# Retention chunks: the group norm moved to POOL and ScalarE one chunk later, PSUM shared out anew, ten modulation rows moved into the loop

## The chip, the core and the metric

The kernel runs on one core of a Trainium2 chip. Its engines work side by side, each through its own instructions in the order in which they were written, and wait for each other by semaphores: PE (TensorE, matrix products out of SBUF into PSUM), DVE (VectorE, elementwise work), ACT (ScalarE, scale, bias, function and copies), POOL (GpSimd, elementwise work in SBUF), and SP, whose queue issues most of the DMAs. PSUM has eight banks of 128 x 512 float32. The metric is the device time of one execution in microseconds; lower is better.

## The reference, cut to what matters

The program is one decoder block on 1024 tokens with a width of 1024: a norm, a token mixer (retention with a gate, and dilated attention), and an MLP. All of it is float32. The change is in the retention, with four heads, chunks of 128 tokens, keys 256 wide and values 512 wide:

```
def step(state, inp):
    qi, ki, vi = inp
    s = jnp.einsum('bhid,bhjd->bhij', qi, ki) * inner_decay[None]
    o = (jnp.einsum('bhij,bhje->bhie', s, vi)
         + jnp.einsum('bhid,bhde->bhie', qi, state) * q_decay[None, :, :, None])
    state = (state * chunk_decay[None, :, None, None]
             + jnp.einsum('bhjd,bhje->bhde', ki * k_decay[None, :, :, None], vi))
    return state, o
...
mu = jnp.mean(ro, axis=-1, keepdims=True)
var = jnp.mean(jnp.square(ro - mu), axis=-1, keepdims=True)
ro = ((ro - mu) * lax.rsqrt(var + GN_EPS)).transpose(0, 2, 1, 3).reshape(B, S, RET_V_W)
ro = (ro * gn_g.astype(jnp.float32) + gn_b.astype(jnp.float32)).astype(h.dtype)
ret_out = (jax.nn.silu(rg) * ro) @ w_ret_out
```

The modulation rows (`mod = silu(c) @ w_ada + b_ada`, 48 columns of 128) are sums of a row of `w_ada` times a vector, made on DVE.

## The kernel before

A float32 product is made of three products of rounded parts: each operand is split into a high part (a rounding copy on ACT) and a low part (a subtraction on DVE), and `mm3` (lines 203 to 211) runs low times high, high times low and high times high, so that one product shows as matmuls of L207, L209 and L211. Each splitting of a 128 x 1024 weight is one ACT copy (L197) and one DVE subtraction (L198).

The order of the instructions is the order of the program text on each engine; nothing reorders them. Steps are run one after the other by `Steps.run`. A step has a list of loads and what is to be done with each when it has come (`wsplit`: split a weight; `mod_load`: one modulation row). SP issues the loads up to three ahead of their use. A chunk's body gets a function `ahead`; where it calls `ahead(2)`, the loads of the next step are prepared, so the splitting and the modulation rows of step g + 1 stand in the engines' order where chunk g calls it.

The stages that matter are `queries_keys` and `values` (lines 1259 and 1384), which end near 712 us, then 32 calls of `chunk(h, c)` (line 715) for head h and chunk c, numbered g = 8 h + c, until near 980 us, then the attention steps. During `queries_keys` and `values`, `mod_turn` (line 1243) loads and sums `NV` = 32 modulation rows in turn, between the other work.

In a chunk TensorE does, in this order: six matmuls for the new state (`kv`, not for c = 7); `RG[h][c] - 1` steps of the gate's projection (`rg_mm`, six matmuls a step; eight steps make a tile of the gate); `s_kt(g + 1)`, the next chunk's scores (`sT`) and transposed keys (`kT`); the chunk's output `o` (nine matmuls, three for c = 0); `on_T(g - 1)`, four transposes (`oT`) of the chunk before, after its norm; one more step of the gate. Around it: DVE brings the state up to date (L745) and takes its low part (L750); ACT takes the high part (L749). In `s_kt` ACT copies the scores out (L652), DVE adds and multiplies by the decay (L653, L654), ACT rounds them (L664), and keys are split (L663, L666). At the end of a chunk DVE takes mean and variance of `o` in PSUM (L772, L773), scales the variance (L774), POOL raises it to -1/2 (L775), DVE scales again (L776) and norms `o` into `onm` (L778). `jit_qk` splits queries and keys on ACT and POOL (L616, L617). For h > 0 and c < 4, `u_final` (line 681) finishes one quarter of the head before: two ACT instructions (L688), one DVE product with the gate (L690), and a store on SP's queue. `rg_out` applies the gate's Silu (L710) when a tile is complete.

PSUM in this stage: the tag `mm` has two slots of two banks (for the gate), the tag `s` four slots of one bank, in which `o` stands beside `kv`, `sT`, `kT` and `oT`.

Of the kernel before, what the change touches and what calls it, by code (L numbers as in the profile page):

```python
# [21 lines left out]
H = 4  # L22
C = 128
NC = S // C
# [13 lines left out]

CS_ID = 0
CS_KDEC = 128  # L40
CS_QD = 132
CS_QD2 = 136
CS_ONE = 140
CS_MH = 141
CS_W = 149
# [95 lines left out]
def block_kernel(ctx, tc, io, stop=None, dbg=None):  # L141
# [3 lines left out]
    def fv(t):  # L145
        return t.bitcast(F32)
# [18 lines left out]

    def ps_mm(name):
        return PS["p"].tile([P, 2, 512], F32, tag="mm", bufs=2, name=name)

    def ps_s(name, shape=(P, 512)):
        return PS["p"].tile(list(shape), F32, tag="s", bufs=PS["n"], name=name)  # L170
# [433 lines left out]
    def flat(ps):  # L604
        return ps.rearrange("p a b -> p (a b)")
# [21 lines left out]
            R[n] = p.tile([P, 2, P], F32R, tag=n, bufs=1, name=n + "00")  # L627
        R["j"] = p.tile([P, 2, 4, C], F32R, tag="j", bufs=2, name="j2")

    def s_kt(i):  # L630

        p = R["p"]
        g = i
        h, c = divmod(g, NC)
        t = hd["j", g]
        ps = ps_s(f"sT{h}{c}")
        for i in range(2):
            nc.tensor.matmul(ps[:, :2 * C], t[:, 0, 2 + i, :], t[:, :, i, :], start=i == 0, stop=False,
                             skip_group_check=True)
            nc.tensor.matmul(ps[:, :C], t[:, 1, 2 + i, :], t[:, 0, i, :], start=False, stop=i == 1,  # L640
                             skip_group_check=True)
# [10 lines left out]
        nc.scalar.copy(sm, ps[:, :C])  # L652
        nc.vector.tensor_add(sm, sm, ps[:, C:2 * C])  # L653
        nc.vector.tensor_mul(sm, sm, decay[:, h * C:(h + 1) * C])  # L654
# [9 lines left out]
        nc.scalar.copy(smh, sm)  # L664
        if pk is not None:
            nc.vector.scalar_tensor_tensor(flat(kl), flat(pk), kd, fv(flat(kh)), op0=ALU.mult, op1=ALU.subtract)  # L666
            hd["k", g] = (kh, kl)
        nc.vector.tensor_sub(sml, sm, fv(smh))

    def on_T(h, c):  # L670

        po = ps_s(f"oT{h}{c}", (P, 4, P))
        on = hd["o", h, c]
        if c == 0:
            hd["on", h] = [etile(f"on{h}{e}") for e in range(4)]
        for e in range(4):
            nc.tensor.transpose(po[:, e, :], on[:, e * P:(e + 1) * P], ident)
        for e in range(4):
            nc.scalar.copy(hd["on", h][e][:, c * C:(c + 1) * C], po[:, e, :])

    def u_final(h, es=range(4), queue=nc.sync):
        for e in es:
            i = h * 4 + e
            t = hd["on", h][e]
            for hf in range(2):
                neg = 16 if hf == i % 2 else 0
                b = t[:, 512 * hf:512 * hf + 512]
                nc.scalar.activation(b, b, AF.Identity, scale=gnv[0][:, neg + i:neg + i + 1],  # L688
                                     bias=gnv[1][:, neg + i:neg + i + 1])
            nc.vector.tensor_mul(t, t, hd["srg", h, e])  # L690
            queue.dma_start(y_d[h][:, 2 * (i % 2):2 * (i % 2) + 2, e // 2], t.rearrange("p (t x) -> p t x", t=2))

    RG = ((6, 2, 2, 3, 3, 3, 3, 2),) + ((3,) * NC,) * (H - 1)

    def rg_mm(n):

        for _ in range(n):
            if hd.get("rgk", NK) == NK:
                hd["rgk"], hd["rgw"], hd["rgp"] = 0, hd["rgws"].pop(0), ps_mm("rg")
            proj_mm(hd["rgp"], hd["rgw"], [hd["rgk"]])  # L700
            hd["rgk"] += 1
            if hd["rgk"] == NK:
                hd["rgs"] = hd["rgp"]

    def rg_out(h, c):

        if "rgs" in hd:
            e = {1: 0, 2: 0, 4: 1, 5: 1, 7: 2}[c]
            hd["srg", h, e] = etile(f"srg{h}{e}")
            nc.scalar.activation(hd["srg", h, e], flat(hd.pop("rgs")), AF.Silu)  # L710
        if c == 6:
            hd["srg", h, 3] = etile(f"srg{h}3")
            nc.sync.dma_start(hd["srg", h, 3], srg_d[h])

    def chunk(h, c, ahead, w=None):
# [18 lines left out]
                kvs.append(kv)  # L734
        if g == 0:
            s_kt(1)
        rg_mm(1 if g == 0 else RG[h][c] - 1)
        for i, kv in enumerate(kvs):
            if g == 0:
                nc.scalar.copy(sh1[:, i, :], kv)  # L740
# [3 lines left out]
            else:  # L744
                nc.vector.scalar_tensor_tensor(st[:, i, :], st[:, i, :], float(GAMMA[h] ** C), kv,  # L745
                                               op0=ALU.mult, op1=ALU.add)
        if g > 0:
            for i in range(len(kvs)):
                nc.scalar.copy(sh1[:, i, :], st[:, i, :])  # L749
                nc.vector.tensor_sub(sl1[:, i, :], st[:, i, :], fv(sh1[:, i, :]))  # L750
# [20 lines left out]
        gr = p.tile([P, 1], F32, tag="gr", bufs=2, name=f"gr{h}{c}")  # L771
        nc.vector.bn_stats(bn, po)  # L772
        nc.vector.bn_aggr(ba, bn)  # L773
        nc.vector.tensor_scalar(gr, ba[:, 1:2], ct[:, CS_QD2 + h:CS_QD2 + h + 1], GN_EPS, op0=ALU.mult, op1=ALU.add)  # L774
        nc.gpsimd.tensor_tensor(gr, gr, mhalf[:, 0:1], op=ALU.pow)  # L775
        nc.vector.tensor_mul(gr, gr, ct[:, CS_QD + h:CS_QD + h + 1])  # L776
        on = p.tile([P, DV], F32, tag="on", bufs=1, name=f"onm{h}{c}")
        nc.vector.tensor_scalar(on, po, ba[:, 0:1], gr, op0=ALU.subtract, op1=ALU.mult)  # L778
# [458 lines left out]
    gate_d = [dram.tile([P, S], F32, name=f"gated{i}") for i in range(16)]  # L1237
    BA = Blocks("qa", XA, ["x"] * 4 + ["wh", "wl"] * 3, lambda kind: True, a_place, a_two, a_temps, a_out)

    NV = 32  # L1240
    turn = {"n": 0, "i": 0}

    def mod_turn():

        turn["n"] += 1
        while turn["i"] < NV + 2 and 7 * turn["n"] > 16 * turn["i"]:
            i = turn["i"]
            turn["i"] += 1
            t = cs[:, i % 2]
            if i > 1:  # L1250
                m = G1 + i - 2
                nc.vector.scalar_tensor_tensor(t, t, 1.0, cb, op0=ALU.mult, op1=ALU.mult, accum_out=mods[:, m:m + 1])
# [1575 lines left out]
def _constants():  # L2828
# [9 lines left out]
    for h in range(H):  # L2838
        lg = math.log(GAMMA[h])
        decay[:, h * C:(h + 1) * C] = \  # L2840
            np.where(i[None, :] >= i[:, None], np.exp(-lg * (i[:, None] + 1)), 0.0) / 16.0
        cst[:, CS_KDEC + h] = np.exp(lg * (C - 1 - i)) / 16.0
        cst[:, CS_QD + h] = np.exp(lg * (i + 1))
        cst[:, CS_QD2 + h] = np.exp(2 * lg * (i + 1))
    cst[:, CS_ONE] = 1.0
    cst[:, CS_MH:CS_MH + 8] = -0.5

# [69 lines left out]
```

## Time and profile before

| | |
|---|---|
| median of 3 runs | 2175.04 us (2174.86 to 2175.66) |
| the profiled execution | 2173.28 us |
| its span in the profile | 2171.3 us |
| around the span | 1.98 us |
| granted TensorE clock | 0.999 |
| retention chunks | about 712 to 980 us |

In the profile a row of the timeline gives start and duration in us, engine, line, operation, tile written <- tiles read, and in brackets how long the engine was idle before it and what released it. A row of the grouped view gives, behind the bar, the time that the group was busy, the mean of one in ns, and the idle time before it. Matmuls overlap each other, so the start of the next one tells more than a duration.

### The profile page before, as it was taken

The page shows a single profiled execution, that of the slowest core. Times are in us where ns is not written, and L with a number is a line of the kernel's source. Part 1 is how long each engine was busy: PE and PEld are TensorE (multiplying, and loading weights), DVE is VectorE, ACT ScalarE, POOL GpSimd, SP SyncE. Part 2 cuts the span into 40 slices and gives each one's busy share as a digit, 9 for nine tenths or more (in the row PEclk, how much of TensorE's full clock was granted, in tenths as well). Part 3 has the DMA queues.
Part 4 walks back from the last instruction along what each step waited for, and adds up shares of the span by engine and source line. Part 5 has one row for each costly group of instructions (what it writes and reads, how often), then busy time and mean ns, then how long its engine had stood idle before and what let it go on. Part 6 is the DMA issues. An engine that isn't in the chain of part 4 may idle for free. (4 is left out here: it accounts for less than half of the span.)

```text
span 2171.3 us, 27289 instructions
## 1 busy us (share of the span) xinstructions
PE 2144.7 (99%) x10036; PEld 1782.4 (82%) x10036; DVE 1520.4 (70%) x2358; ACT 959.3 (44%) x1757; POOL 165.7 (8%) x199
## 2 busy tenths in 40 slices
PE   8999999999999999999999999999999999999998
PEld 6888888888887788888888888888778888888887
DVE  6886777777656677776667644677876665877855
ACT  5543322323334455556656625434454455533413
POOL 0001111100001112211110000001000000000003
PEclk9999999999999999999999999999999999999999
DMA  9859998835588744436877366653144435645322
GB/s 383 282 208 309 285 306 265 243 117 194 186 301 303 234 148 151 160 127 197 218 194 196 115 245 211 217 191 132 64 175 160 150 136 193 253 135 173 109 88 78
DMA packets 162674, 425.18 MB, mean 196 GB/s; under 512 B 28005, under 2 KB 55916, under 8 KB 159468
## 3 DMA queue, kind: packets, MB, share of 16 engines
q1 hardware_dynamic: 150264, 374.90, 48.3%
q0 software_dynamic: 9584, 48.24, 9.9%
q8 instruction: 79, 1.29, 0.2%
q10 hardware_dynamic: 2692, 0.30, 0.1%
q14 instruction: 55, 0.45, 0.1%
HBM read 324.13 MB, written 160.32 MB: 223 GB/s over the span
## 5 line engine op out<-in xcount | busy, mean ns | idle before, releaser
L207 PE MATMUL qap<-hh,qaw 128*128 128x512 f32 x264 | 102.7, 389 | 0.0
L209 PE MATMUL qap<-hl,qaw 128*128 128x512 f32 x264 | 102.7, 389 | 0.0
L211 PE MATMUL qap<-hh,qaw 128*128 128x512 f32 x264 | 102.7, 389 | 0.0
L617 POOL TENSOR_TENSOR j<-qk,j 128x512 fp32r<-128x512 f32 x32 | 42.8, 1338 | 454.8 <-ACT j L616 454.8
L2235 POOL TENSOR_TENSOR accnf<-accnf,sqnf 128x256 f32<-128x256 f32 (+1 forms) x18 | 16.6, 922 | 609.6 <-ACT sqnf L2231 609.6
L2339 ACT ACTIVATE a<-a 128x512 f32<-128x512 f32 x48 | 30.3, 631 | 72.8 <-DVE a L2338 71.3
L749 ACT CAST stateh<-state 128x512 fp32r<-128x512 f32 x54 | 32.9, 622 | 57.8 <-DVE state L745 55.7
L209 PEld LDWEIGHTS qap<-hl,qaw 128*128 128x128 f32 x264 | 49.5, 188 | 10.4
L211 PEld LDWEIGHTS qap<-hh,qaw 128*128 128x128 f32 x264 | 49.6, 188 | 10.3
L207 PEld LDWEIGHTS qap<-hh,qaw 128*128 128x128 f32 x264 | 49.5, 188 | 10.2
L2547 ACT CAST w2h<-w2s 128x512 fp32r<-128x512 f32 x36 | 22.4, 621 | 80.3 <-DVE w2s L2585 80.3
L264 DVE TENSOR_TENSOR fw<-w1r,fw 128x512 fp32r<-128x512 f32 x48 | 32.9, 688 | 33.6 <-ACT fw L254 33.6
L264 DVE TENSOR_TENSOR qaw<-wa,qaw 128x512 fp32r<-128x512 f32 x66 | 44.0, 687 | 9.4 <-ACT qaw L254 9.4
L2070 DVE TENSOR_TENSOR rwl<-rwl,rwh 128x1024 fp32r<-128x1024 f32 x25 | 30.2, 1221 | 29.0 <-ACT rwh L2100 29.0
L207 PE MATMUL fp<-h2h,fw 128*128 128x512 f32 x128 | 50.0, 390 | 0.0
L209 PE MATMUL fp<-h2l,fw 128*128 128x512 f32 x128 | 49.8, 389 | 0.0
L211 PE MATMUL fp<-h2h,fw 128*128 128x512 f32 x128 | 49.8, 389 | 0.0
L207 PE MATMUL roa<-rh,rwl 128*128 128x512 f32 x128 | 49.8, 389 | 0.0
L209 PE MATMUL roa<-rl,rwh 128*128 128x512 f32 x128 | 49.8, 389 | 0.0
L211 PE MATMUL roa<-rh,rwh 128*128 128x512 f32 x128 | 49.8, 389 | 0.0
L1603 ACT ACTIVATE P<-P,ng 128x128 f32<-128x128 f32 (+1 forms) x96 | 41.9, 438 | 17.6 <-DVE ng L1595 17.5
L292 DVE TENSOR_TENSOR qat<-qat,qap 128x512 f32<-128x512 f32 x22 | 15.1, 688 | 42.8 <-PE qap L211 35.8
(3089 smaller groups left out, 7187.8 us busy)
## 6 DMA issues: line engine op xcount, KB each, us to landing
cossin<-in_w_ada_dram SPq DMA_DIRECT2D x32, 512.0 KB, 3.5
v<-vd SPq DMA_DIRECT2D x32, 512.0 KB, 4.3
w1r<-in_w_ff_dram SPq DMA_DIRECT2D x32, 512.0 KB, 4.6
yt<-y POOLq DMA_DIRECT2D x24, 512.0 KB, 7.5
xsd<-as SPq DMA_DIRECT2D x24, 512.0 KB, 3.1
w2r<-in_w_ff2s_dram SPq DMA_DIRECT2D x24, 512.0 KB, 6.4
em<-in_w_ada_dram SPq DMA_DIRECT2D x16, 512.0 KB, 10.2
wrvs<-in_w_rv_dram POOLq DMA_DIRECT2D x16, 512.0 KB, 9.8
```

Source lines behind the costliest of these rows:

```text
L207: nc.tensor.matmul(o, wl, xh, start=first, stop=False, skip_group_check=skip)
L209: nc.tensor.matmul(o, wh, xl, start=False, stop=False, skip_group_check=skip)
L211: nc.tensor.matmul(o, wh, xh, start=False, stop=last, skip_group_check=skip)
L264: nc.vector.tensor_sub(t[:, 512:], src, fv(t[:, :512]))
L292: nc.vector.tensor_sub(u, u, b)
L617: nc.gpsimd.tensor_sub(t[:, 1], src, fv(t[:, 0]))
L749: nc.scalar.copy(sh1[:, i, :], st[:, i, :])
L1603: nc.scalar.activation(v, v, AF.Exp, bias=ng[:, blk:blk + 1], accum_out=st[:, g, blk, 2 + a:3 + a])
L2070: nc.vector.tensor_sub(lo, fv(lo), fv(hi))
L2235: (nc.vector if f == 7 else nc.gpsimd).tensor_add(G["acc", key], G["acc", key], sq)
L2339: nc.scalar.activation(o, o, AF.Relu)
L2547: nc.scalar.copy(hi, src)
```

## The change

The group norm of chunk g is no longer done by DVE at the end of chunk g. There DVE makes mean and variance and adds a constant; POOL makes three 128 x 1 operations (minus the mean, the power, their product); and ScalarE applies scale and bias out of PSUM in chunk g + 1, after `s_kt(g + 2)` and before `on_T(g)`. The last chunk does it at once. The decay factor of the query goes into the epsilon, so the two constants' columns are other ones.

`o` and the gate get PSUM tags of their own, with two banks each (`ps_o`, `ps_rg`); four banks remain for `s`. The gate's tile was two slots of two banks and is now one pair of banks. The Silu follows at once on the tile's last step, in two halves. A new `banks(False)` stands at the start of the attention. The low part of the state's first half moves into `s_kt`, that of the second half to after the norm's statistics; `ahead(2)` moves from before `s_kt` to after them (in the last chunk it stays where it was). The DVE product and the store of `u_final` come one chunk later than its two ACT instructions. `on_T` copies with two instructions of 128 x 256 in place of four of 128 x 128. `RG` for heads 1 to 3 goes from 3 in each chunk to (3, 3, 2, 3, 3, 2, 4, 4), whose sum is the same. A weight of the gate belongs to the step before the one that first uses it (steps 0, 1, 4, 7, 10, 13, 15, 18, 21, 23, 26, 29). `NV` goes from 32 to 22, `mod_turn` takes a row every 2 turns, where it was 16/7, and the ten rows left become loads of the steps 6, 12, 13, 14, 20, 21, 22, 28, 29 and 30.

```diff
+    def ps_rg(name):
+        return PS["p"].tile([P, 512], F32, tag="rg", bufs=2, name=name)
+    def ps_o(name):
+        return PS["p"].tile([P, 512], F32, tag="o", bufs=2, name=name)
...
-        return R["p"].tile([P, 1024], dt, tag="E", bufs=12, name=name)
+        return R["p"].tile([P, 1024], dt, tag="E", bufs=4, name=name)
...
-    def s_kt(i):
+    def s_kt(i, mid=None):
...
+        if mid:
+            mid()
         nc.vector.tensor_sub(sml, sm, fv(smh))
...
-            hd["on", h] = [etile(f"on{h}{e}") for e in range(4)]
+            hd["on2", h] = [R["p"].tile([P, 2, 1024], F32, tag="EO", bufs=4, name=f"on{h}{e}") for e in range(2)]
+            hd["on", h] = [hd["on2", h][e // 2][:, e % 2] for e in range(4)]
...
-        for e in range(4):
-            nc.scalar.copy(hd["on", h][e][:, c * C:(c + 1) * C], po[:, e, :])
+        for e in range(2):
+            nc.scalar.copy(hd["on2", h][e][:, :, c * C:(c + 1) * C], po[:, 2 * e:2 * e + 2, :])
...
-            nc.vector.tensor_mul(t, t, hd["srg", h, e])
-            queue.dma_start(y_d[h][:, 2 * (i % 2):2 * (i % 2) + 2, e // 2], t.rearrange("p (t x) -> p t x", t=2))
-    RG = ((6, 2, 2, 3, 3, 3, 3, 2),) + ((3,) * NC,) * (H - 1)
+            def mul(t=t, i=i, e=e):
+                nc.vector.tensor_mul(t, t, hd["srg", h, e])
+                queue.dma_start(y_d[h][:, 2 * (i % 2):2 * (i % 2) + 2, e // 2], t.rearrange("p (t x) -> p t x", t=2))
+            if late:
+                return mul
+            mul()
+    RG = (6, 2, 2, 3, 3, 3, 3, 2), (3, 3, 2, 3, 3, 2, 4, 4), (3, 3, 2, 3, 3, 2, 4, 4), (3, 3, 2, 3, 3, 2, 4, 4)
...
-                hd["rgk"], hd["rgw"], hd["rgp"] = 0, hd["rgws"].pop(0), ps_mm("rg")
+                hd["rgk"], hd["rgw"], hd["rgp"] = 0, hd["rgws"].pop(0), [ps_rg(f"rg{i}") for i in range(2)]
...
-                hd["rgs"] = hd["rgp"]
+                i = hd["rgi"] = hd.get("rgi", -1) + 1
+                t = hd["srg", i // 3, i % 3] = etile(f"srg{i // 3}{i % 3}")
+                for j, ps in enumerate(hd["rgp"]):
+                    nc.scalar.activation(t[:, 512 * j:512 * j + 512], ps, AF.Silu)
...
-        rg_mm(1 if g == 0 else RG[h][c] - 1)
+        rg_mm(1 if g == 0 else RG[h][c] - (g < NG - 1))
...
-        if g > 0:
-            for i in range(len(kvs)):
+        def low(i):
+            nc.vector.tensor_sub(sl1[:, i, :], st[:, i, :], fv(sh1[:, i, :]))
+        if g > 0 and kvs:
+            for i in range(2):
                 nc.scalar.copy(sh1[:, i, :], st[:, i, :])
-                nc.vector.tensor_sub(sl1[:, i, :], st[:, i, :], fv(sh1[:, i, :]))
...
-        ahead(2)
+        if g == NG - 1:
+            ahead(2)
         if 0 < g < NG - 1:
-            s_kt(g + 1)
-        po = ps_s(f"o{h}{c}")
+            s_kt(g + 1, (lambda: low(0)) if kvs else None)
+        if "onm" in hd:
+            hd.pop("onm")()
+        po = ps_o(f"o{h}{c}")
...
-        rg_mm(0 if g == 0 else 1)
+        rg_mm(1 if 0 < g < NG - 1 else 0)
...
-        nc.vector.tensor_scalar(gr, ba[:, 1:2], ct[:, CS_QD2 + h:CS_QD2 + h + 1], GN_EPS, op0=ALU.mult, op1=ALU.add)
-        nc.gpsimd.tensor_tensor(gr, gr, mhalf[:, 0:1], op=ALU.pow)
-        nc.vector.tensor_mul(gr, gr, ct[:, CS_QD + h:CS_QD + h + 1])
+        nc.vector.tensor_scalar_add(gr[:, 0:1], ba[:, 1:2], ct[:, CS_EQ + h:CS_EQ + h + 1])
+        nc.gpsimd.tensor_tensor(gr[:, 2:3], ba[:, 0:1], ct[:, CS_NEG:CS_NEG + 1], op=ALU.mult)
+        nc.gpsimd.tensor_tensor(gr[:, 1:2], gr[:, 0:1], mhalf[:, 0:1], op=ALU.pow)
+        nc.gpsimd.tensor_tensor(gr[:, 2:3], gr[:, 1:2], gr[:, 2:3], op=ALU.mult)
+        if g > 0 and kvs:
+            low(1)
+        if g < NG - 1:
+            ahead(2)
+        if "um" in hd:
+            hd.pop("um")()
+        if h > 0 and c < 4:
+            hd["um"] = u_final(h - 1, (c,), late=True)
         on = p.tile([P, DV], F32, tag="on", bufs=1, name=f"onm{h}{c}")
-        nc.vector.tensor_scalar(on, po, ba[:, 0:1], gr, op0=ALU.subtract, op1=ALU.mult)
+        hd["onm"] = lambda: nc.scalar.activation(on, po, AF.Identity, scale=gr[:, 1:2], bias=gr[:, 2:3])
+        if g == NG - 1:
+            hd.pop("onm")()
...
-        if h > 0 and c < 4:
-            u_final(h - 1, (c,))
...
-    NV = 32
+    NV = 22
...
-        while turn["i"] < NV + 2 and 7 * turn["n"] > 16 * turn["i"]:
+        while turn["i"] < NV + 2 and turn["n"] > 2 * turn["i"]:
...
+    RGW, n = [], 0
+    for g in range(NG):
+        RGW += [g - (g > 1)] * (n < 8 * len(RGW) + 1 <= n + RG[g // NC][g % NC])
+        n += RG[g // NC][g % NC]
+    late_mods = iter(range(G1 + NV, 48))
...
-                      ([wsplit(io["w_rg"][3 * h + (0, 2, 5).index(c)])] if c in (0, 2, 5) else []),
+                      ([wsplit(io["w_rg"][RGW.index(NC * h + c)])] if NC * h + c in RGW else []) +
+                      ([mod_load(next(late_mods))] if NC * h + c == 6 or h > 0 and c in (4, 5, 6) else []),
...
     def att_step(pair, a):
         def body(*args):
+            if pair == a == 0:
+                banks(False)
```

More of the change, by code (lines that the diff above doesn't have):

```diff
@@ L40 @@
 CS_KDEC = 128
-CS_QD = 132
-CS_QD2 = 136
+CS_NEG = 132
+CS_EQ = 136
 CS_ONE = 140
@@ L674, in on_T, with u_final @@
         if c == 0:
-            hd["on", h] = [etile(f"on{h}{e}") for e in range(4)]
+            hd["on2", h] = [R["p"].tile([P, 2, 1024], F32, tag="EO", bufs=4, name=f"on{h}{e}") for e in range(2)]
+            hd["on", h] = [hd["on2", h][e // 2][:, e % 2] for e in range(4)]
         for e in range(4):
             nc.tensor.transpose(po[:, e, :], on[:, e * P:(e + 1) * P], ident)
-        for e in range(4):
-            nc.scalar.copy(hd["on", h][e][:, c * C:(c + 1) * C], po[:, e, :])
-    def u_final(h, es=range(4), queue=nc.sync):
+        for e in range(2):
+            nc.scalar.copy(hd["on2", h][e][:, :, c * C:(c + 1) * C], po[:, 2 * e:2 * e + 2, :])
+    def u_final(h, es=range(4), queue=nc.sync, late=False):
         for e in es:
@@ L702, in rg_mm @@
             if hd["rgk"] == NK:
-                hd["rgs"] = hd["rgp"]
+                i = hd["rgi"] = hd.get("rgi", -1) + 1
+                t = hd["srg", i // 3, i % 3] = etile(f"srg{i // 3}{i % 3}")
+                for j, ps in enumerate(hd["rgp"]):
+                    nc.scalar.activation(t[:, 512 * j:512 * j + 512], ps, AF.Silu)
     def rg_out(h, c):
[L707 to L710, printed above, removed]
         if c == 6:
@@ L767, in chunk @@
             on_T(*divmod(g - 1, NC))
[L768 removed]
+        rg_mm(1 if 0 < g < NG - 1 else 0)
         bn = p.tile([P, 6], F32, tag="bn", bufs=2, name=f"bn{h}{c}")
         ba = p.tile([P, 2], F32, tag="ba", bufs=2, name=f"ba{h}{c}")
[L771 removed]
+        gr = p.tile([P, 3], F32, tag="gr", bufs=2, name=f"gr{h}{c}")
         nc.vector.bn_stats(bn, po)
         nc.vector.bn_aggr(ba, bn)
[L774 to L776 removed]
+        nc.vector.tensor_scalar_add(gr[:, 0:1], ba[:, 1:2], ct[:, CS_EQ + h:CS_EQ + h + 1])
[10 more added lines that the diff above has]
+            hd["um"] = u_final(h - 1, (c,), late=True)
         on = p.tile([P, DV], F32, tag="on", bufs=1, name=f"onm{h}{c}")
[L778 removed]
+        hd["onm"] = lambda: nc.scalar.activation(on, po, AF.Identity, scale=gr[:, 1:2], bias=gr[:, 2:3])
+        if g == NG - 1:
+            hd.pop("onm")()
         hd["o", h, c] = on
         rg_out(h, c)
[L781 to L782 removed]
     def wsplit(ap):
@@ L2842, in _constants @@
         cst[:, CS_KDEC + h] = np.exp(lg * (C - 1 - i)) / 16.0
-        cst[:, CS_QD + h] = np.exp(lg * (i + 1))
-        cst[:, CS_QD2 + h] = np.exp(2 * lg * (i + 1))
+        cst[:, CS_NEG] = -1.0
+        cst[:, CS_EQ + h] = GN_EPS * np.exp(-2 * lg * (i + 1))
     cst[:, CS_ONE] = 1.0
```

## The prediction, made before the changed kernel was run

> **What bounds the kernel now.** I read the page first, then TensorE's waits between 600 and 1000 us, then the engines' shares by stage, and last single chunks.
>
> ```profile
> span 2171.3 us, 27289 instructions
> ...
> PE 2144.7 (99%) x10036; PEld 1782.4 (82%) x10036; DVE 1520.4 (70%) x2358; ACT 959.3 (44%) x1757; POOL 165.7 (8%) x199
> ```
>
> TensorE is busy for 2144.7 of 2171.3 us. That alone doesn't say that it runs without holes, since matmuls overlap in these records, so I went by its waits. In the stretch that the change touches these are the larger ones (engine, line, who was waited for, us in all, times, longest):
>
> ```profile
> PE vc L209 <- DVE vwl L1328: 1.9, 2, 1.5
> PE rg L207 <- DVE vr L1367: 1.1, 1, 1.1
> PE kv L207 <- ACT state L763: 0.9, 1, 0.9
> ```
>
> ```profile
> 650.00:700.00 50.00, 48.08 (x211) 39.15 (x210) 35.22 (x47) 23.61 (x36) 4.81 (x4) 1.00 0.79 295
> ...
> 850.00:900.00 50.00, 49.95 (x250) 41.65 (x249) 40.11 (x84) 29.39 (x72) 10.76 (x12) 1.00 0.48 155
> ```
>
> All three stand before 726 us: two in the values stage, one where the first gate tile takes over PSUM, one in the second chunk. In the chunks proper, here 850 to 900, TensorE is busy for 49.95 of 50 us, while DVE has 10 and ACT 20 us to spare. So the loop of chunks has next to nothing to give, and whatever the new order makes TensorE wait for is lost in full. The question is therefore not how much work DVE loses but whether the norm, which is now made in the chunk where TensorE wants it, comes in time.
>
> **The change part by part.** Durations, grouped over the chunks (715 to 985 us):
>
> ```profile
> L750 DVE TENSOR_TENSOR statel<-state,stateh 128x512 fp32r<-128x512 f32 x54 | 35.0, 689 | 2.5
> L745 DVE SCALAR_TENSOR_TENSOR state<-state,kv 128x512 f32<-128x512 f32 x48 | 30.6, 680 | 0.0
> L778 DVE TENSOR_SCALAR onm<-o,ba,gr 128x512 f32<-128x512 f32 x32 | 25.9, 810 | 3.4
> L772 DVE BATCH_NORM_STATS2 bn<-o 128x6 f32<-128x512 f32 x32 | 22.3, 696 | 10.3 <-PE o L211 10.3
> L690 DVE TENSOR_TENSOR on<-on,srg 128x1024 f32<-128x1024 f32 x12 | 14.6, 1219 | 0.1
> ...
> L774 DVE TENSOR_SCALAR gr<-ba,ct 128x1 f32<-128x1 f32 x32 | 6.9, 214 | 1.1
> ...
> L198 DVE TENSOR_TENSOR raw_5955l<-raw,raw_5955h 128x1024 fp32r<-128x1024 f32 x1 | 1.2, 1228 | 0.2 <-ACT raw_5955h L197 0.2
> ```
>
> ```profile
> L749 ACT CAST stateh<-state 128x512 fp32r<-128x512 f32 x54 | 32.9, 622 | 57.8 <-DVE state L745 55.7 <-DVE state L743 2.0
> L679 ACT COPY on<-oT 128x128 f32<-128x128 f32 x124 | 23.8, 277 | 13.3 <-PE oT L677 13.3
> L688 ACT ACTIVATE on<-on,gnt 128x512 f32<-128x512 f32 x24 | 18.6, 838 | 0.0
> ...
> L710 ACT ACTIVATE srg<-rg 128x1024 f32<-128x1024 f32 x12 | 12.6, 1050 | 3.1 <-PE rg L211 3.1
> ...
> L763 ACT COPY state<-kv 128x512 f32<-128x512 f32 x2 | 1.1, 584 | 0.0
> L197 ACT CAST raw_5359h<-raw 128x1024 fp32r<-128x1024 f32 x1 | 1.1, 1052 | 0.0
> ```
>
> ```profile
> L617 POOL TENSOR_TENSOR j<-qk,j 128x512 fp32r<-128x512 f32 x30 | 38.8, 1292 | 203.7 <-ACT j L616 203.7
> L775 POOL TENSOR_TENSOR gr<-gr,ct 128x1 f32<-128x1 f32 x32 | 17.5, 546 | 15.2 <-DVE gr L774 15.2
> ```
>
> *Amounts.* DVE loses the norm, 25.9/32 = 0.81 us a chunk, and L776; it gains ten modulation rows. ACT gains the norm. The nearest row is L688, the same shape with scale and bias by partition, 18.6/24 = 0.78 us; the bounds are 0.58 (a copy out of PSUM, L763) and 0.81 (DVE's own). I take 0.78, because L688 has the same two operands. The Trainium skill, page "ScalarE: Activation LUTs", section "What ACT_TABLE_LOAD costs", gives 186 ns plus 0.833 ns per element, 93 ns more for each operand by partition, and an overlap of 93 ns between neighbours. By that a norm would be an estimated 0.71 us behind another instruction, which would make each stall below 0.07 us shorter; L688 agrees within that. POOL's three small operations cost 3 x 0.55 us behind its 1.29 us; they have a chunk's time, and cost nothing unless a chunk were under some 4 us. Two copies in place of four save ACT at most 0.4 us a chunk. The Silu in halves costs at most one instruction's start more, some 0.1 us. The stores of y come a chunk later, on SP's queue, and nothing reads them before the attention. The TensorE work is the same: the new `RG` has the same sum.
>
> *When the norm can come.* Two views of the second chunk's scores, where no engine was behind:
>
> ```profile
> 721.41 0.28 PE L638 MATMUL sT<-j 128*128 128x256 f32 x1
> ```
> ```profile
> 722.02 0.27 ACT L652 COPY sm<-sT 128x128 f32<-128x128 f32 x1 [4.83 <-PE sT L640]
> ...
> 722.97 0.30 ACT L664 CAST smh<-sm 128x128 fp32r<-128x128 f32 x1 [0.24 <-DVE sm L654]
> ```
>
> From the first score matmul to the end of ACT's rounding (L664) is 723.27 - 721.41 = 1.86 us, since that copy needs L652 on ACT and L653 and L654 on DVE. The norm stands right behind it in ACT's order: it ends 1.86 + 0.78 = 2.64 us after the scores begin, less some 0.05 of overlap, plus the signal: 2.6. When does TensorE want it?
>
> ```profile
> 822.09 0.60 PE L677 MATMUL oT<-ct,onm 128*128 128x128 f32 x4
> ...
> 823.92 0.39 PE L207 MATMUL kv<-v,kl 128*128 128x512 f32 x1
> ...
> 825.28 0.62 PE L207 MATMUL rg<-hh,raw_5684l 128*128 128x512 f32 x2
> ...
> 828.00 0.28 PE L638 MATMUL sT<-j 128*128 128x256 f32 x1
> ...
> 830.73 0.60 PE L677 MATMUL oT<-ct,onm 128*128 128x128 f32 x4
> ```
>
> ```profile
> 852.41 0.28 PE L638 MATMUL sT<-j 128*128 128x256 f32 x1
> ...
> 853.75 0.60 PE L677 MATMUL oT<-ct,onm 128*128 128x128 f32 x4
> ```
>
> In a plain chunk oT follows the scores by 830.73 - 828.00 = 2.73 us: the norm comes 0.1 us early, at no cost. In a chunk with c = 0 there are three output matmuls in place of nine, and the distance is 1.34 us. So TensorE stands for 2.6 - 1.34 = **1.3 us** at c = 0 of heads 1, 2 and 3.
>
> *When DVE or ACT is behind.* I count from the start of oT (t = 0). From the rows above, kv starts at 1.83, takes 1.36, each gate step takes 1.36 (the row at 828.00 is two steps after 825.28), so the scores start at 5.91 with two gate steps in front, and at 4.55 with one. One is what the new `RG` leaves in front at c = 2 and c = 5 of heads 1 to 3, and there oT is due at 4.55 + 2.73 = 7.28.
>
> ```profile
> 830.93 0.70 DVE L772 BATCH_NORM_STATS2 bn<-o 128x6 f32<-128x512 f32 x1 [0.51 <-PE o L211]
> ```
>
> ```profile
> 831.37 0.78 ACT L679 COPY on<-oT 128x128 f32<-128x128 f32 x4 [0.47 <-PE oT L677]
> ```
>
> DVE starts the statistics at 0.2 and with L772 (0.70) and two small ones (0.2 each, L774) is done at 1.35; the low half (35.0/54 = 0.65) ends at 2.0. ACT starts its two copies at 0.64 and is free at 1.4. What comes next is what moved behind the norm's statistics:
> - c = 2: at the end of c = 1 a weight is split (copy 1.05, to 2.45; L198 1.22, to 3.7), then the gate product of `u_final` (1.22, to 4.9), then the two state updates (2 x 0.64, to 6.15). ACT's second high part (0.61) ends at 6.75; only then come L652, and 1.25 us later the end of L664 (723.27 - 722.02), then the norm: 8.7. Against 7.28, **1.4 us**.
> - c = 5: at the end of c = 4 both a weight and a modulation row stand there (steps 13, 21, 29): 3.7, then 1.22 and a small sum to 5.1, the product to 6.3, the states to 7.6, ACT's high part to 8.2, the norm at 10.2. Against 7.28, **2.9 us**.
> - c = 4 has a row and the product, but two gate steps: the states end at 5.9, ACT's high part at 6.5, when the scores' copy could start anyway (5.91 + 0.61). Nothing, with 0.1 to spare. The other chunks have less.
>
> Per head 1.3 + 1.4 + 2.9 = 5.6 us, three heads: **16.8**. In head 0 there is no `u_final`, and nothing is late but chunk 1, below.
>
> *The last chunk.* Four gate steps come in front, then the two Silus (1.05), then `ahead(2)` with a weight's copy (1.05), then the norm of chunk 30 (0.78): with 0.2 us for the first Silu to start, 3.1 us after the gate's end. The nine output matmuls take 2.73 less the scores' 0.55, so 2.2. **+0.9**. Bounds 0 and 1.3, the latter if the weight's low part is late too.
>
> *The gate's single pair of banks.* A tile ends with the chunk; the next one starts behind six kv matmuls, 1.36 us later, its second bank 0.23 later. The Silus need 0.2 + 1.05 us, plus one start. Fits by some 0.2; cost 0, and 0.3 for each of 11 tiles if ACT is behind.
>
> *The start.* kv's wait for L763 (0.9) goes, since `o` no longer takes one of the four slots. But the first weight's splitting now stands in front of the states of chunk 1, and its norm is due after one gate step: by the same sums oT begins about 1 us later than before, while the small waits of chunk 2 go. **0**, bounds -1.5 and +2.5.
>
> *The values stage.* The two waits of 1.9 us in all are DVE being behind:
>
> ```profile
> 649.41 0.60 ACT L1362 ACTIVATE vo<-va 128x512 fp32r<-128x512 f32 x1 [4.44 <-DMA vd<-vo]
> ```
>
> ```profile
> 650.65 1.22 DVE L1252 SCALAR_TENSOR_TENSOR cossin<-cossin,cb 128x1024 f32<-128x1024 f32 x1
> ...
> 653.77 1.22 DVE L1328 TENSOR_TENSOR vwl<-vwl,vwh 128x1024 fp32r<-128x1024 f32 x1
> ```
>
> ACT and then DVE had waited 4.4 us for a slot that a store to HBM still held, and a modulation row (1.22 us) stands ahead of the late low parts. After the change the last row is summed at turn 47 (24 x 2 - 1), of which 38 lie before the values stage and 40 in it, so both the row and part of the transfers are gone: **-1.9**, bounds 0 and -2.4. The 1.1 us at the first gate tile are mostly the last value's own subtraction; **-0.3**, bounds 0 and -1.1. What hid the ten rows before, free DVE time, is missing only at c = 5, where they are counted.
>
> **Sum:** 16.8 + 0.9 + 0 - 1.9 - 0.3 = +15.5 us on the profiled execution's 2173.28 (span 2171.3 and 1.98 around it), 2188.8. That execution is 1.76 below the median, so the forecast for the median is 2175.04 + 15.5 = 2190.5.
>
> **Rivals.**
> - *Relief without a new wait.* If ACT gets to the norm before TensorE gets to oT (because score copy and rounding are faster behind each other than I think, or DVE's backlog shorter), only gains are left: 1.9 + 1.1 + 0.9 = 3.9, and perhaps 1 of tiny waits: -5, so 2170. For it: DVE and ACT have time to spare on average. Against it: spare time on average is no use where three things stand in a row in front of the states, and at c = 0 no backlog is needed.
> - *Only c = 0 stalls.* If DVE is not behind at c = 2 and c = 5, 3.9 + 0.9 - 2.2 = +2.6: 2177.6, no change that could be told.
> - *The gate's banks too.* If Silus come behind other ACT work, 11 x 0.3, and the plain chunks lose their 0.1 us and 0.1 more, 24 x 0.1: +6 on the forecast: 2196.
> - *The first weight's splitting doesn't come sooner.* It is written behind a slot that the first values still hold; then chunk 1 costs up to 2.5 more, 2193. This lies within the forecast's range.
>
> **How the numbers follow.** Forecast 0.70 with its like (the last rival in it), the gate's banks too 0.07, c = 0 alone 0.09, relief 0.14. What a measurement of this kernel can tell from no change is about 0.2%, 4.4 us. So slower 0.77, within 0.09, faster 0.14. The forecast's own range: each stall 0.3 shorter or longer (ten of them, 3 us), the start -1.5 to +2.5, values 0 to -2.4: 2185 to 2197. To hold 8 in 10 the range reaches down into the case of c = 0 alone: 2175 to 2197.
>
> **What would show it.** TensorE should wait at oT for ACT's norm some ten times, 15 to 20 us in all, longest near 3 us at c = 5 of heads 1 to 3; in the other chunks oT should follow the scores by 2.73 us as before. The vc waits should be gone. If TensorE's waits for the norm sum to under 5 us, the order on ACT and DVE was misread; if the time is up without them, look at the gate's first matmul after a Silu, or at DMA waits of the ten rows on DVE.

## The result, and the profile after

| | before | after |
|---|---|---|
| median | 2174.93 us (2173.19 to 2175.66, 6 runs) | 2189.40 us (2184.66 to 2190.38, 6 runs) |
| the profiled execution | 2173.28 us | 2190.38 us |
| granted TensorE clock in it | 0.999 | 0.996 |

The kernel became slower: after over before is 1.0063, with a 95% interval from 1.005 to 1.0076, 14.5 us between the medians.

The head of the page after:

```profile
span 2188.6 us, 27342 instructions
...
PE 2149.7 (98%) x10036; PEld 1785.1 (82%) x10036; DVE 1499.1 (68%) x2304; ACT 980.0 (45%) x1737; POOL 210.8 (10%) x263
```

DVE is busy for 21 us less than before and ACT for 21 us more; the span is 17.3 us longer. TensorE's waits from 600 to 1000 us, after (engine, line, who was waited for, us in all, times, longest):

```profile
PE oT L686 <- ACT onm L806: 15.3, 11, 2.2
PE rg L213 <- DVE vr L1395: 0.8, 1, 0.8
```

The waits of the values stage and of the second chunk are gone. In their place there is one new wait, eleven times: the transposes (oT) wait for ScalarE's norm (onm). Two of the places in TensorE's timeline after, c = 0 and c = 5 of head 1:

```profile
783.69 0.28 PE L644 MATMUL sT<-j 128*128 128x256 f32 x1
...
786.32 0.66 PE L686 MATMUL oT<-ct,onm 128*128 128x128 f32 x4 [1.13 <-ACT onm L806]
...
825.31 0.28 PE L644 MATMUL sT<-j 128*128 128x256 f32 x1
...
830.44 0.66 PE L686 MATMUL oT<-ct,onm 128*128 128x128 f32 x4 [2.24 <-ACT onm L806]
```

oT follows the scores by 2.63 and 5.13 us, where the work between them takes 1.34 and 2.73 by the rows of before: 1.3 and 2.4 us are lost. (I count this way, from start to start; the bracket counts from the modelled end of the last matmul and gives less.) Counted so, the eleven are: c = 0 of three heads 1.30 each, c = 2 1.07 each, c = 5 2.4 each, chunk 1 of head 0 2.13, the last chunk 0.69; 17.1 us in all.

What ACT and DVE do ahead of the norm at c = 5, in their timelines after:

```profile
823.02 1.22 DVE L204 TENSOR_TENSOR raw_6171l<-raw,raw_6171h 128x1024 fp32r<-128x1024 f32 x1
824.16 1.22 DVE L470 SCALAR_TENSOR_TENSOR raw<-raw,cb 128x1024 f32<-128x1024 f32 x1
...
825.50 1.22 DVE L701 TENSOR_TENSOR on<-on,srg 128x1024 f32<-128x1024 f32 x1
826.64 1.28 DVE L759 SCALAR_TENSOR_TENSOR state<-state,kv 128x512 f32<-128x512 f32 x2
```

```profile
827.35 1.22 ACT L766 CAST stateh<-state 128x512 fp32r<-128x512 f32 x2 [4.36 <-DVE state L759]
828.47 0.26 ACT L658 COPY sm<-sT 128x128 f32<-128x128 f32 x1
...
829.41 0.30 ACT L670 CAST smh<-sm 128x128 fp32r<-128x128 f32 x1 [0.30 <-DVE sm L660]
829.61 0.77 ACT L806 ACTIVATE onm<-o,gr 128x512 f32<-128x512 f32 x1
```

This is the chain that the prediction laid out: weight, modulation row, gate product, two states on DVE, then high parts, scores' copy, rounding and norm on ACT. ACT was idle for 4.36 us ahead of it. POOL's timeline after shows when the norm's scale and bias were there:

```profile
823.04 1.61 POOL L795 TENSOR_TENSOR gr<-gr,ct 128x1 f32<-128x1 f32 x1
824.73 0.71 POOL L796 TENSOR_TENSOR gr<-gr 128x1 f32<-128x1 f32 x1
```

They were there at 825.44, 4.2 us before the norm starts: it stood behind instructions that weren't ready, while its own inputs were.

One thing was not in the prediction. The windows view after, in three stretches of 3.41 us around chunk 1's wait (busy time and count of PE, PEld, DVE, ACT, POOL, then the granted clock, the DMA share and GB/s):

```profile
725.76:729.18 3.42, 1.46 (x9) 0.99 (x8) 2.50 (x8) 2.88 (x8) 0.31 (x1) 1.00 0.89 275
729.18:732.59 3.41, 3.41 (x10) 2.64 (x9) 1.49 (x3) 1.59 (x4) 2.28 (x4) 0.50 1.03 350
732.59:736.00 3.41, 3.41 (x19) 2.90 (x19) 1.82 (x4) 1.90 (x4) 0.00 (x0) 1.00 0.19 57
```

TensorE waits through much of the first stretch; in the second it is granted half its clock and gets through 10 matmuls in place of 19, though it counts as busy all the time. Such stretches begin at 729.18, 831.58 and 903.26 us, each after one of the long waits, and cost an estimated 1.7 us each (half of 3.41), 5 us in all. The third wait at c = 5 (head 3), 2.40 us like the others, has none behind it.

### The profile page after: what moved, and what is told of

The parts are those of the page before. It is cut to its first block, busy times and chain, and to the rows that moved or that the text cites. A ratio compares the mean times of both kernels' runs of the same rounds, so it can differ in the third digit from the quotient of the medians.

```text
span 2188.6 us, 27342 instructions
## 1 busy us (share of the span) xinstructions
PE 2149.7 (98%) x10036; PEld 1785.1 (82%) x10036; DVE 1499.1 (68%) x2304; ACT 980.0 (45%) x1737; POOL 210.8 (10%) x263
## 5 line engine op out<-in xcount | busy, mean ns | idle before, releaser
L659 DVE TENSOR_TENSOR sm<-sm,sT 128x128 f32<-128x128 f32 x32 | 9.2, 288 | 69.4 <-ACT sm L658 69.4
```

## The experiments

Diffs are against the changed kernel unless it is said. Theory A is the prediction's: the norm comes late because of where it stands in ACT's order, behind the scores' copies and with them behind DVE's backlog. Each ratio is to runs of the kernel before on the same chip, whose medians were 2174.41 to 2174.71 us.

**The norm in front of the state update** (`e1_norm_first`).

```diff
+        if "onm" in hd:
+            hd.pop("onm")()
         for i, kv in enumerate(kvs):
...
-        if "onm" in hd:
-            hd.pop("onm")()
         po = ps_o(f"o{h}{c}")
```

> The changed kernel with one edit: ScalarE makes the norm of chunk g-1 before the state's high parts and the next chunk's scores, in place of behind them. Theory A (the time is lost because the norm stands behind the scores' copies, and these behind DVE's backlog): TensorE's waits at oT for onm fall from 15.3 us to under 1, the three stretches of half clock behind long waits (some 5 us in the profiled run) go with them, and the time falls by 17 to 22 us to 2167 to 2172, below the kernel before. Rival B (the norm on POOL and ScalarE is late by itself, whatever stands in front of it, because POOL's three operations and a ScalarE pass take longer than a chunk gives): the waits at oT stay above 10 us and the time stays above 2184. Rival C (the two banks for the gate cost as much): the oT waits go, but waits at rg for ACT's srg come in their place, and the time stays above 2178.

Measured: 2171.06 us (2170.2 to 2171.96, 11 runs), 0.9983 of before [0.9974, 0.9992]. Its waits from 600 to 1010 us, the larger two:

```profile
PE ak L213 <- DVE raw_8173l L204: 1.3, 1, 1.3
PE rg L213 <- DVE vr L1395: 0.8, 1, 0.8
```

No wait at oT is left, and no stretch of half clock in the chunks. One moved statement takes 18.3 us off the changed kernel. What is new against the changed kernel is a wait in the attention's first step for a weight split in the last chunk (1.3 us). The gate's single pair of banks, a rival, shows up in three gaps of 0.25 us and no more.

**The ten rows back in the values stage** (`e2_rows_back`).

```diff
-    NV = 22
+    NV = 32
...
-        while turn["i"] < NV + 2 and turn["n"] > 2 * turn["i"]:
+        while turn["i"] < NV + 2 and 7 * turn["n"] > 16 * turn["i"]:
```

The chunks' steps load no rows.

> The changed kernel with the ten modulation rows back in the earlier stages (NV = 32 and the old rate, no such loads in the chunks). Theory A: the row is one of three things on DVE in front of the states at c = 5, so the wait there falls from 2.4 us each to 1.0 to 1.2, while c = 0 (1.3) and c = 2 (1.1) stay; the half clock after c = 5 goes; the vc waits of the values stage (1.9 us, 2.2 by the gaps between matmuls) come back. Time: -3.7 for c = 5, -1.7 for each half clock that goes (0 to 2 of them), +4 for the values stage: 2185 to 2189. Rival (the rows hide in DVE's spare time and c = 5 is late for another reason, one gate step in front): c = 5 keeps 2.2 to 2.4 us, and the time rises to 2191 or more.

Measured: 2184.94 us (2184.76 to 2187.71, 5 runs), 1.0052 [1.004, 1.0065]. The larger two of its waits from 600 to 1010 us:

```profile
PE oT L686 <- ACT onm L806: 11.9, 11, 2.6
PE vc L215 <- DVE vwl L1356: 2.1, 2, 1.5
```

The stall at c = 5 fell from 2.4 to 1.06 us, nearly that of c = 2, which together with c = 0 stayed as it was. So the row accounts for 1.3 us of each c = 5, one L470 and its small sum. The vc waits of before are back, so they were the rows' doing. Chunk 1's wait, about which nothing was expected, grew from 2.13 to 2.72 us; why is open. No stretch of half clock is left.

**The gate's product one step later** (`e3_product_later`): `um` is popped after `s_kt`, ahead of the norm.

```diff
-        if "um" in hd:
-            hd.pop("um")()
...
+        if "um" in hd:
+            hd.pop("um")()
         if "onm" in hd:
```

> The changed kernel with DVE's product of the head before (and its store) behind the next chunk's scores, in place of ahead of the state updates. Theory A: it takes 1.2 us out of what stands in front of the states at c = 2 and c = 5 of heads 1 to 3, so c = 2 falls from 1.1 to under 0.4 and c = 5 from 2.4 to about 1.2, while c = 0 stays at 1.3 and chunk 1 of head 0 at 2.1. Time: -2.1 to -3.2 for c = 2, -3.6 for c = 5, and the half clock after c = 5 (1.7 us each, 0 to 2) goes: 2180 to 2185. Rival (ACT's own queue, not DVE's, holds the norm up): c = 2 and c = 5 stay within 0.3 us of what they are, and so does the time.

Measured: 2183.87 us (2181.84 to 2184.66, 5 runs), 1.0043 [1.003, 1.0055]. c = 2 fell from 1.07 to 0.51, c = 5 from 2.4 only to 1.89, where about 1.2 was expected. Its DVE timeline near c = 5 tells why:

```profile
821.48 1.22 DVE L701 TENSOR_TENSOR on<-on,srg 128x1024 f32<-128x1024 f32 x1
822.61 0.69 DVE L793 BATCH_NORM_STATS2 bn<-o 128x6 f32<-128x512 f32 x1
```

The product now stands ahead of the statistics of the chunk before, which it delays by 0.9 us: DVE's line in front of the states holds the same instructions. Of the 0.5 us that are gained about half is the time in which DVE had waited for `o`; the other half is the state's low part, which holds DVE for 0.59 us in place of 0.84. The time lies in the expected range, but the size at c = 5 was missed; the theory stands.

**The rows alone, on the kernel before** (`e4_rows_alone`): before, with `NV = 22`, a row every two turns and the ten rows in the chunks' steps.

> The kernel before with only the modulation rows moved (NV = 22, a row every 2 turns, ten rows as loads of chunk steps 6, 12, 13, 14, 20, 21, 22, 28, 29, 30). Theory A: the values stage loses its waits (2.2 us at vc by the gaps, 0.9 at va, 0.3 at the first gate tile, and the slow matmuls behind them) and the loop of chunks, where the norm is made a chunk ahead of its use, hides the rows in DVE's spare time: 3 to 5 us faster than the kernel before, 2170 to 2172. Rival (ten rows of 1.4 us on DVE make kv wait for the split keys, as they make the norm late in the changed kernel): waits at kv for kl of 0.5 us or more in the chunks c = 3 to 5, and no gain or a loss, 2174 to 2180.

Measured: 2177.27 us (2176.23 to 2179.8, 11 runs), 1.0014 [1.0005, 1.0023], where 2170 to 2172 was expected: the rival held. From 600 to 1010 us its largest wait is:

```profile
PE kv L207 <- DVE kl L666: 4.9, 4, 1.6
```

The values stage's waits went, but in three chunks with both a weight and a row TensorE now waits for the keys' low part. In the kernel before, the rows' move loses 2.6 us; with the norm first on ACT it gains (seventh experiment). That it pays only with the norm off DVE is likely, but no run shows that alone.

**The last chunk's weight earlier** (`e5_last_split`): the first experiment, with

```diff
+        if g == NG - 1:
+            ahead(2)
         rg_mm(1 if g == 0 else RG[h][c] - (g < NG - 1))
```

in place of the call that stood behind the state update.

> The version with the norm first, and in the last chunk the split of the attention's first weight ahead of the gate's steps, in place of behind them. In the run with the norm first TensorE waited 1.3 us (1.5 by the gaps) at ak for that split. Theory A (the split is late only because two Silus and the norm stand in front of its copy on ScalarE): that wait goes and nothing takes its place: 1.3 to 1.6 us under that run, 2169 to 2170. Rival (the weight itself comes late from HBM, or oT of the last chunks then waits for the norm): the wait stays above 1 us or an oT wait of 0.7 or more comes back, and the time stays at 2171.

Measured: 2169.72 us (2168.19 to 2171.19, 11 runs), 0.9978 [0.9969, 0.9986]. The wait of 1.3 us is gone.

**Waits made longer on purpose** (`e6_long_waits`): the first experiment, but in eleven chunks the norm is late again, behind 4, 5 or 6 ScalarE copies that nobody reads.

```diff
+            for _ in range(LATE[g]):
+                nc.scalar.copy(cs[:, 1, :512], cs[:, 0, :512])
```

> The version with the norm first, except in 11 chunks (c = 1, 3, 4; not c = 1 of head 0), where the norm stays behind the next chunk's scores and ScalarE makes 4, 5 or 6 copies of 128x512 ahead of it that nothing uses. They make TensorE wait at oT about 2.0, 2.5 and 3.0 us. Theory H, from the runs so far: the clock goes to a half for one window of 3.413 us when TensorE stood for more than 2.04 to 2.16 us within the window before it, on a fixed grid of windows; so a wait of 2.0 never does it, and one of 2.5 or 3.0 does it where at least 2.1 us of it lie in one window, which is some half of the 2.5 ones and two thirds of the 3.0 ones: 3 to 7 half-clock windows, all behind such waits and all on one grid. Rival 1 (the length of the wait alone decides, near 2.1 us): every wait of 2.5 and 3.0 is followed by half clock, 8 windows. Rival 2 (only a window with TensorE idle throughout, 3.4 us, lowers the clock, and the three in the changed kernel's profile had another cause): none. Time: 11 waits of 27 us in all on top of 2171, and 1.7 us for each half-clock window: 2201 to 2212.

Measured: one run of 2217.8 us, above what was expected, since the waits came out 0.3 to 0.6 us longer (2.33, 3.04 and 3.63 us) and there were nine stretches of half clock. All eight waits of 3.0 and 3.6 us were followed by one, and of three waits of 2.33 us only the first. Two of these three, by windows of one grid of 3413.33 ns on which all nine begin:

```profile
800.91:804.32 3.41, 1.27 (x8) 1.15 (x9) 1.69 (x4) 3.11 (x8) 0.74 (x1) 1.00 0.00 0
804.32:807.73 3.41, 3.41 (x10) 2.67 (x9) 2.37 (x3) 3.14 (x5) 2.24 (x4) 0.50 0.00 0
879.41:882.83 3.42, 1.65 (x8) 0.99 (x6) 2.99 (x8) 3.09 (x7) 0.00 (x0) 1.00 0.00 0
882.83:886.24 3.41, 3.01 (x16) 2.57 (x17) 0.86 (x2) 3.17 (x7) 2.40 (x4) 1.00 0.00 0
```

The two waits are equally long; with 1.27 us busy in the window the next one has half the clock, with 1.65 it hasn't. So length alone doesn't decide, and the window needn't be idle throughout: in the chunks it is how much of one fixed window TensorE was idle. In this run it was busy for 1.27 us or less in the window ahead of each half clock, and for 1.65 or more in all other windows there.

**The first experiment with the rows back** (`e7_first_rows_back`): the edits of the first and the second together.

> The version with the norm first and the ten modulation rows back in the earlier stages. Theory A (with the norm out of the way of DVE's backlog, moving the rows is a gain, since the chunks hide them and the values stage loses its waits; and that is the larger part of what the version with the norm first gains on the kernel before): the waits at vc come back, 3 to 5 us slower than with the norm first: 2174 to 2176. Rival (the rows moved cost about what they save, as they did when moved alone in the kernel before): within 1 us of the version with the norm first.

Measured: 2172.58 us (2171.43 to 2174.63, 11 runs), 0.9991 [0.9982, 1.0]. The larger two of its waits from 600 to 1010 us:

```profile
PE rg L213 <- DVE vr L1395: 1.7, 1, 1.7
PE vc L215 <- DVE vwl L1356: 1.5, 1, 1.5
```

2.4 us more of these two than in the first experiment, but only 1.5 us more in the median, where 3 to 5 were expected. From the first vc to the gate's first matmul it takes 114.15 us, 4.2 more than the first experiment's 109.94; from there to the attention's first (ak) 266.63, 1.4 less than 267.99. So in these two executions the rows' move saves 4.2 us in the values stage and costs 1.4 in the chunks. The median moves by 1.5; what takes the rest isn't shown.

**The norm back on DVE** (`e8_norm_on_vector`): the changed kernel, but DVE norms at the end of the chunk, and POOL does only the power.

```diff
-        hd["onm"] = lambda: nc.scalar.activation(on, po, AF.Identity, scale=gr[:, 1:2], bias=gr[:, 2:3])
...
+        nc.vector.tensor_scalar(on, po, ba[:, 0:1], gr[:, 1:2], op0=ALU.subtract, op1=ALU.mult)
```

> The changed kernel with the norm on DVE at the end of its own chunk, behind the split, the modulation row and the product, and POOL doing the power alone; all else as changed. Theory A (DVE is what stands in front of everything, so 0.8 us more on it comes out where the states are late): no waits at oT, but at c = 5 of heads 1 to 3, where split, row, product and now the norm precede the states, the next chunk's keys are split late and kv waits 1 to 2 us for kl; 2172 to 2177, slower than with the norm first on ScalarE. Rival (DVE has the time, and moving the norm to ScalarE is worth nothing): no wait above 0.5 us in the chunks and a time within 1 us of 2171.

Measured: 2173.34 us (2172.48 to 2174.57, 11 runs), 0.9995 [0.9987, 1.0004]. TensorE waits 1.5 us in all, four times, for the keys' low part, less than expected. So the rest of the change is no loss (the interval holds 1); the late norm is.

**The gate's steps as before** (`e9_gate_even`): `(3,) * NC` in heads 1 to 3.

> The changed kernel with the gate's steps as before, three in each chunk of heads 1 to 3; the norm stays behind the scores. Theory A (c = 2 and c = 5 are late because DVE's and ACT's backlog meets one gate step in front of the scores, and c = 0 because three output matmuls stand there in place of nine): with two steps in front, 1.36 us more time, the wait at c = 2 goes (1.07, under 0.2 left) and that at c = 5 falls from 2.4 to about 1.0; c = 0 stays at 1.3, chunk 1 of head 0 at 2.1. Gate tiles now end in the middle of a chunk, so at most 0.3 us each may come at rg. Time: 3 x 1.07 + 3 x 1.36 = 7.3 us less and no half clock behind c = 5: 2179 to 2183. Rival (the wait at c = 2 and c = 5 belongs to the chunk's other work and moves with it): both stay within 0.3 us of what they are, 2185 to 2190.

Measured: 2188.0 us (2184.23 to 2188.22, 5 runs), 1.0055 [1.0043, 1.0068], against 2179 to 2183 expected. The edit moves more than the gate's steps: `RGW` is worked out from `RG`, so six weights of the gate are now split one chunk earlier (steps 9, 12, 17, 20, 25 and 28, where they were 10, 13, 18, 21, 26 and 29). The wait at c = 5 is gone, and one of 1.06 us stands at c = 4, which had none: there weight, row and product now meet two gate steps. That is Theory A's order, at a place that I hadn't foreseen. c = 2 has no weight in front any more and still waits 1.23 us. ACT's timeline there:

```profile
800.63 1.09 ACT L721 ACTIVATE srg<-rg 128x512 f32<-128x512 f32 x2 [3.19 <-PE rg L217]
801.60 1.14 ACT L766 CAST stateh<-state 128x512 fp32r<-128x512 f32 x2
802.63 0.28 ACT L658 COPY sm<-sT 128x128 f32<-128x128 f32 x1
...
803.79 0.77 ACT L806 ACTIVATE onm<-o,gr 128x512 f32<-128x512 f32 x1
```

With this distribution a tile of the gate ends in front of c = 2's scores, and its two Silus stand on ACT ahead of the state's high parts, the scores' copy and the norm. At c = 5, where the next tile ends, TensorE also waits for the single pair of banks (1.4 us over three times). I had looked at DVE's backlog alone.

**The norm at the end of its own chunk** (`e10_same_chunk`): still POOL and ScalarE, but not one chunk later.

```diff
-        if "onm" in hd:
-            hd.pop("onm")()
         po = ps_o(f"o{h}{c}")
...
-        if g == NG - 1:
-            hd.pop("onm")()
+        hd.pop("onm")()
```

> The changed kernel with the norm still on POOL and ScalarE, but made at the end of its own chunk, as the last instruction of the chunk on ScalarE. Theory A (what costs is the place behind the scores, not POOL or ScalarE): no waits at oT; ScalarE stands until POOL's product is done, some 4 us into the next chunk, and the states' high parts follow, which is still before the scores in most chunks: 2170 to 2173. Rival (ScalarE, held up by POOL, is late with the scores and the split keys): waits at kv for kl or kh of 0.5 us or more in several chunks, 2175 to 2182.

Measured: 2169.64 us (2169.08 to 2173.84, 11 runs), 0.9979 [0.997, 0.9988]. The larger waits left from 600 to 1010 us:

```profile
PE rg L213 <- DVE vr L1392: 0.8, 1, 0.8
PE ak L213 <- DVE raw_8173l L204: 0.7, 1, 0.7
```

Without the delay the change is 4.8 us faster than before, and 3.7 us faster than with the norm on DVE (another chip; 3.5 by the two ratios): taking the norm off DVE does pay. With the fifth experiment this is the fastest; the two can't be told apart.

## Why the prediction was right

2190.5 us was forecast, 2189.4 measured, with the predicted cause. That the total came out within 1.1 us is in part luck: the sum has misses that offset each other.

| term | predicted, us | measured, us |
|---|---|---|
| c = 0, three heads | 3 x 1.3 | 3 x 1.30 |
| c = 2, three heads | 3 x 1.4 | 3 x 1.07 |
| c = 5, three heads | 3 x 2.9 | 3 x 2.4 |
| last chunk | +0.9 | +0.69 |
| start, chunk 1 | 0 | +2.1 for the norm, some 2.7 of before's waits there gone |
| values stage | -1.9 | -3.7 |
| gate's first tile | -0.3 | -0.3 |
| half clock | not foreseen | some +5 |

- *The order of the chain* held at each place, and the first and the tenth experiments show that it is the whole loss: with the norm elsewhere in the order all eleven waits go. The plain chunks had their 0.1 us, as forecast: no wait there.
- *c = 2 and c = 5* were mis-sized by 0.3 and 0.5. I added durations end to end. In the rows above, instructions of 1.22 us start 1.14 apart (823.02, 824.16): about 0.08 of each lies beside the next, over the six or seven that stand in a row. The term for c = 0 was taken from start times, and came out right. The norm itself was 774 ns, against 0.78 taken.
- *Chunk 1* does wait, by twice what I put for the later start of oT; that it nets to nothing holds only as to idle time. The rival about this chunk's first weight isn't what happened: ACT copies it at 722.23 us without idle time ahead of it.
- *The values stage* gave more than the waits view showed. In the windows from 600 to 712 us, before:

```profile
600.00:712.00 112.00, 108.84 (x475) 88.43 (x473) 67.85 (x94) 46.42 (x69) 8.33 (x10) 1.00 0.83 310
```

and after:

```profile
600.00:712.00 112.00, 111.22 (x491) 91.75 (x490) 56.98 (x72) 47.53 (x70) 7.13 (x10) 1.00 0.78 279
```

TensorE is busy for 2.4 us more, while DVE is busy for 11 us less. From the stage's first vc matmul to the gate's first matmul it takes 113.83 us before (598.60 to 712.43) and 109.76 after (599.29 to 709.05): 4.1 less, 0.3 of it at the gate's first tile, and so 3.7 for the stage, many gaps being too small for the waits view. The term was half of that.
- *The missing term* is the clock, 5 us. It made up for stalls that I had put 2.7 us too large (17.7 against 15.0) and a values stage put 1.8 too small. From the gate's first matmul to the attention's first it takes 268.32 us before (712.43 to 980.75) and 287.72 after (709.05 to 996.77): 19.4 more, which is 17.1 of waits and 5 of clock less the 2.7 of before's waits. With 4.1 less in front of it, 0.7 more up to the first vc (a load at the start, 0.6) and 1.3 more from the attention on (one wait at 1853 us, 1.0, which not all kernels with the same code there show) this is the 17.3 us between the spans. The 14.5 us between the medians are less, since the profiled execution after is the slowest of its six, and that of before is faster than its median.
- *The gate's pair of banks* didn't decide: three gaps of 0.25 us in the first experiment, nothing that stands out in the changed kernel; only in the ninth, where tiles end in the middle of a chunk, does it cost 1.4 us. The rival "c = 0 alone" fell with c = 5, "relief" with all eleven.

## What to carry to other kernels

A step that is put off belongs in front of the work that its engine is still waiting for, not behind it: being ready is of no use to an instruction that stands behind others which are not, and here one statement's place was worth 18 us. Cost a deferred step at its narrowest place (the chunk with the least work between, the chunk with the longest backlog), not on an average chunk, where it fitted with 0.1 us to spare. On a bound TensorE, count a stall of 2 us and more with what the clock may take after it.

## What the hardware showed that was not expected

**The clock is lowered for one whole window after a window with enough idle time.** In the changed kernel and in the sixth experiment the matmuls' spacing nearly doubles (427 ns in place of 227) for 3.413 us. The Trainium skill, page "TensorE: Matmul & The Clock Gate", Part 1, gives a free-running window of 4096 cycles at 1.2 GHz, 3413 ns, and these runs agree with it: the starts lie on one grid of that step. For the drop it names at least one idle window of some 3.4 us, and here the runs differ: in the twelve traces, from 20 us after the start to 20 us before the end, each window of the grid in which TensorE was busy for 1.46 us or less was followed by half clock, and none in which it was busy for 1.65 or more. In the last 20 us idle time by this view isn't the measure: in the eighth experiment the clock falls after a window with 2.51 us busy, but 1.2 of these are eight 128 x 1 products.

The grid lies elsewhere in each execution: with whole windows taken off, the stretches begin at 2.14 us in the changed kernel, 0.64 in the third experiment and 1.35 in the ninth. So the same wait costs 1.7 us more or nothing by where it falls. Of the three equal waits at c = 5 the last lies across two windows, with 2.37 and 2.21 us busy. That is likely why the changed kernel's runs spread over 5.7 us (2184.66 at a clock of 0.998, 2190.38 at 0.996), and before's over 2.5; with six runs this is argued, not shown.

**A tiny POOL power took 0.54 or 1.5 to 1.6 us, by whether DVE had begun ahead of it.** POOL's groups in the chunks, after:

```profile
L795 POOL TENSOR_TENSOR gr<-gr,ct 128x1 f32<-128x1 f32 x31 | 34.5, 1114 | 0.1
L794 POOL TENSOR_TENSOR gr<-ba,ct 128x1 f32<-128x1 f32 x31 | 17.6, 568 | 7.0 <-DVE ba L792 7.0
```

The power took 546 ns on average before, and 1114 here, but that mean mixes two sizes. Seventeen of the 31 took 1.53 us or more: each begins less than 0.1 us behind the start of a 128 x 1024 DVE instruction with two operands in SBUF (L204, L470 or L701), and ends 0.4 us behind its end. At c = 5 it ran 1.61 us, from 823.04, behind the L204 of 823.02. At c = 2 it began just ahead of the same kind of L204, and took 0.54:

```profile
797.27 0.54 POOL L795 TENSOR_TENSOR gr<-gr,ct 128x1 f32<-128x1 f32 x1
797.29 1.24 DVE L204 TENSOR_TENSOR raw_5902l<-raw,raw_5902h 128x1024 fp32r<-128x1024 f32 x1
```

In the tenth experiment it took 0.54 too where it began just behind L759, which reads PSUM. DVE's low parts of the state were slower, 822 ns against 689:

```profile
L762 DVE TENSOR_TENSOR statel<-state,stateh 128x512 fp32r<-128x512 f32 x54 | 44.4, 822 | 0.0
```

In the tenth experiment the power took 786 ns on average and that subtraction 685. That one waits for the other is read from the order of the starts; no experiment isolates it. It cost nothing here, since the norm waited for ACT's order anyway.
